# First-layer queries, decayed products and decay rows in DRAM tiles of their own, 2 KB per partition

## The chip, the cores and the metric

The kernel runs on one core of one Trainium2 chip. The metric is the device time of one execution in microseconds (us). For the kernel before, three runs gave 1664.18 us as the median, 1661.94 to 1669.47.

## The reference, cut to what matters

Three blocks work on 512 tokens (16 meta tokens ahead of them) of width 1024: a gated delta-rule layer, a latent-attention layer, and a layer of pooling, dilated attention and a feed-forward part. The change touches the first layer alone. It has 8 query/key heads of 128 features, each shared by 2 of the 16 value heads. In chunks it computes

```
gc = jnp.cumsum(g, axis=-1)
decay = jnp.exp(jnp.where(incl, gc[..., :, None] - gc[..., None, :], -jnp.inf))
attn = jnp.einsum('bhnid,bhnjd->bhnij', q, k) * decay
...
v_new = u_c - jnp.einsum('bhcd,bhde->bhce', w_c, state)
o_c = jnp.einsum('bhcd,bhde->bhce', qd_c, state) + jnp.einsum('bhij,bhje->bhie', a_c, v_new)
state = state * gl_c[..., None, None] + jnp.einsum('bhcd,bhce->bhde', kd_c, v_new)
```

The queries `q`, the decayed products `attn` and the rows of `gc` that `decay` is made from are what the change stores elsewhere. In the kernel a chunk is 128 tokens: chunk 0 holds the 16 meta tokens, chunks 1 to 4 the others.

## The kernel before, in words

Every projection is a product in three passes (high and low halves of both sides, lines 68, 71 and 72) that accumulates in PSUM tiles `pj_t`. Its weights come in units of 128x1024 floats (512 KB) from DRAM through line 115, and ScalarE (line 78) and VectorE (line 79) cut them in two. `first_layer` works in this order: gates and keys, half of the output gates, the 8 query heads, the 16 value heads, the other output gates, and then `core`, the recurrence over the chunks.

Nearly all loads and stores are issued by SyncE, which takes them in one fixed order. What stands in that order behind a transfer that waits, waits too. The order of each engine comes from a scheduler at build time. Side work (Gram products, decayed products, joins) runs as generators that are stepped with a budget between the halves of a projection (`column_tiles`, `bg.run`).

**Decay rows.** `decay_rows` (line 798) transposes `gc` into 80 rows of 128 floats (5 chunks by 16 heads) and stores them as `row_a`, one after another. Later `scores` (line 1093) loads, for each query head and each pair of chunks, the rows of its 2 value heads in both chunks to all 128 partitions at once (`fetch`, line 1100; tile `bca`). In `row_a` the two heads of a chunk are neighbours, and the two chunks lie 8 KB apart.

**Decayed products.** `products` masks `bca` on GpSimd (line 1109), takes exponents on ScalarE (line 1115), multiplies queries by keys on TensorE (`gq`, line 1117), joins both on VectorE (line 1118), and the result goes to DRAM (line 1129), in two pieces per partition: those of each chunk stand in another slab of `item_dram`. There are 2 such rounds per head, 16 in all. `bca` has 4 buffers (pool `ew`, tag `bc`), so the fifth load waits until the first store has landed.

**Queries.** `query_norm` (line 1079) stores each head's queries, four pieces of 128 floats per partition, into the same slabs (line 1080).

**Items.** `item_dram[u]` so holds for head `u` and chunk `c` one slab of 128 partitions by 768 floats: values and keys (384, line 1151), decayed products (256), queries (128). In `core` the stage `prepare` (line 1220) fetches such a slab in one transfer (line 1224) into one of 5 `item` buffers. `from_state` uses its queries two turns later (`ks`, line 1295), `new_values` follows, and `update` uses keys and decayed products (lines 1325 and 1333). A turn handles one of 32 pairs of chunk and head; the load of a turn waits for line 1325 of the item five turns before. `update` also loads the gates `sz` (line 1338). From the 24th turn on the next layer's output projection fills TensorE beside it.

```
stages = ((prepare, 0), (from_state, 2), (new_values, 3), (update, 4), (gated, 7))
```

Of the kernel before, what the change touches and what calls it, by code (L numbers as in the profile page):

```python
# [12 lines left out]
F32 = mybir.dt.float32  # L13
# [7 lines left out]
P = 128  # L21
D = 1024
KT = 8
META = 16
SEQ = 512
# [195 lines left out]
def tile_model(ctx, tc, a, out):  # L221
# [64 lines left out]
    with ExitStack() as mixed:  # L286
        ghi, glo, core = first_layer(e, mixed)
        mix = Mix(e, mixed, "w_out0", 2, None, "post0", HALVES, ghi, glo, (a["x0"], a["x1"]))
        half = mix.first_half()
        core(half)  # L290
        for _ in half:
            pass
        second = Second(e)
        mix.run(second)
# [255 lines left out]
def first_layer(e, mixed):  # L550
    tc, nc, a, dram, pj, wts, bg, ident, ones, vcol = (
        e.tc, e.nc, e.a, e.dram, e.pj, e.wts, e.bg, e.ident, e.ones, e.vcol
    )
    sz_dram = dram.tile([16, P, T1], F32, name="sz_dram")

    item_dram = [dram.tile([5, P, 6 * P], F32, name=f"item_dram{u}") for u in range(8)]
    row_a = dram.tile([80, P], F32, name="row_a")
    row_b = [dram.tile([40, P], F32, name=f"row_b{i}") for i in range(2)]

    left, right = ExitStack(), ExitStack()  # L560
# [25 lines left out]
    for i, s in enumerate(HALVES):  # L586
        x = flat[:, KT * s.start:KT * s.stop].rearrange("p (k t) -> p k t", k=KT)
# [164 lines left out]
    u = gs.tile([P, 5, 32], F32, name="u")  # L752
# [45 lines left out]
    def decay_rows():  # L798
        ra = gs.tile([80, P], F32, tag="ra", name="ra")
        ps = tr_tile([P, P], "ra_ps")  # L800
        nc.tensor.transpose(ps[0:80], gc.rearrange("p c h -> p (c h)"), ident)
        nc.vector.tensor_copy(ra, ps[0:80])
        nc.sync.dma_start(row_a, ra)
        nc.sync.dma_start(bc0, row_a[0:16, 0:META].partition_broadcast(META))

    one = gs.tile([P, 31], F32R, name="one")
    zero = gs.tile([P, 31], F32, name="zero")
# [5 lines left out]
    def square_sums(src, j, n, then):  # L813

        sq = cv.tile([P, T1], F32, tag="sq", name="sq")
        sqhi = cv.tile([P, T1], F32R, tag="sqhi", name="sqhi", bufs=1)
        sqlo = cv.tile([P, T1], F32R, tag="sqlo", name="sqlo", bufs=1)
        nc.scalar.activation(sq, src, AF.Square)
        cut(nc, sqhi, sqlo, sq)

        def sums():
            if j == 0:
                ss_t[0] = psm.tile([2 * n, CUT], F32, tag="ss", name="ss")
            for i, s in enumerate(HALVES):
                at = j + n * i
                for x in (sqhi, sqlo):
                    nc.tensor.matmul(
                        ss_t[0][:, 0:s.stop - s.start], lhsT=one[:, 15 - at:15 - at + 2 * n], rhs=x[:, s],
                        start=(at == 0 and x is sqhi), stop=(at == 2 * n - 1 and x is sqlo), skip_group_check=True,
                    )  # L830
            if j == n - 1:
                rows = gs.tile([2 * n, CUT], F32, tag="ssr", name="ssr")
                nc.scalar.activation(rows, ss_t[0], AF.Copy)
                side.add(1.5, lambda: columns(rows))

        def columns(rows):
            ps = tr_tile([P, 5, 2 * n], "ss_c")
            for c in range(5):
                t = win(c).start
                i = t >= CUT  # L840
                t -= HALVES[i].start
                nc.tensor.transpose(ps[:, c], rows[:, t:t + P], ident[0:2 * n, 0:2 * n])
            for cs, i in ((slice(0, 3), 0), (slice(3, 5), 1)):
                then(cs, ps[:, cs, n * i:n * i + n])

        side.add(SUMS, sums)
# [230 lines left out]
    bc0 = gs.tile([META, 16, META], F32, name="bc0")  # L1077

    def query_norm(kh, qT):
        nc.sync.dma_start(  # L1080
            item_dram[kh][1:5, :, 5 * P:].rearrange("c p t -> p c t"), qT[:, META:].rearrange("p (c t) -> p c t", t=P)
        )
        bg.add(scores(kh, qT), P_EARLY)

        def then(cs, ps):
            nc.vector.tensor_scalar(
                out=qe[:, :, cs].rearrange("p k c -> p c k"), in0=ps, scalar1=P * EPS, scalar2=P * EPS * EPS,
                op0=ALU.mult, op1=ALU.add,
            )

        square_sums(qT, kh, 8, then)

    def scores(kh, qT):

        hs = slice(2 * kh, 2 * kh + 2)
        rows = row_a.rearrange("(c h) i -> c h i", h=16)

        def fetch(c):
            bc = ew.tile([P, 2, 2, P], F32, tag="bc", name="bca")
            nc.sync.dma_start(  # L1100
                bc.rearrange("p j h i -> p j (h i)"),
                rows[c:c + 2, hs].rearrange("c h i -> c (h i)").partition_broadcast(P),
            )
            return bc

        def products(ex, rows, cs, n):
            ps = gr_tile([P, 2, P], "gq")
            for j, c in enumerate(cs):
                nc.gpsimd.affine_select(
                    out=ex[:, j], in_=rows[:, j], pattern=[[0, 2], [1, n]], compare_op=ALU.is_ge,  # L1110
                    fill=NEG, base=0, channel_multiplier=-1,
                )
                for r in range(2):
                    h = 2 * kh + r
                    nc.scalar.activation(ex[:, j, r], ex[:, j, r], AF.Exp, bias=col[0:n, c, h:h + 1])
                ts = slice(CHUNKS[c][0], CHUNKS[c][0] + n)
                nc.tensor.matmul(ps[0:n, j, 0:n], lhsT=kT[:, kh, ts], rhs=qT[:, ts], start=True, stop=True)
            nc.vector.tensor_tensor(
                out=ex, in0=ps[0:n, 0:len(cs), 0:n].unsqueeze(2).broadcast_to([n, len(cs), 2, n]), in1=ex, op=ALU.mult
            )  # L1120

        todo = (1, 3)
        ahead = deque(fetch(c) for c in todo)
        products(at0[:, hs].unsqueeze(1), bc0[:, hs].unsqueeze(1), (0,), META)
        yield 0.3, 0
        for c in todo:
            ex = ahead.popleft()
            products(ex, ex, (c, c + 1), P)
            nc.sync.dma_start(
                item_dram[kh][c:c + 2, :, 3 * P:5 * P].rearrange("c p a -> p c a"), ex.rearrange("p c r i -> p c (r i)")  # L1130
            )
            yield 2 * PRODUCT + 0.15, 0

    def token_rows(u, vT, c):
# [22 lines left out]
    def gates_later():  # L1157
        side.add(2.0, gates)
        side.add(10.0, cumulate)
        side.add(14.0, decay_rows)  # L1160
# [59 lines left out]
    def prepare(c, u):  # L1220
        o = live[c, u] = Env()
        item = ahead.tile([P, 6, P], F32, tag="item", name="item", bufs=5)
        o.vb, o.at, o.q = item[:, 0:3], item[:, 3:5], item[:, 5]
        nc.sync.dma_start(item.rearrange("p a d -> p (a d)"), item_dram[u][c])

    nothing = lambda: None
    keys = [conv_silu(("w_k", kh), 8 + kh, kT[:, kh], K_BUDGET, lambda kh=kh: key_norm(kh)) for kh in range(2)]
# [18 lines left out]
    for kh in range(8):  # L1246
        qT = cv.tile([P, T1], F32, tag="vT", name="qT", bufs=5)
        column_tiles(conv_silu(("w_q", kh), kh, qT, Q_BUDGET, lambda kh=kh, qT=qT: query_norm(kh, qT)))
# [23 lines left out]
    for i in range(5):  # L1272
        prepare(1, i)
# [68 lines left out]
    def gated(c, u):  # L1342
# [12 lines left out]
        cut(nc, ghi[i][:, us, ts], glo[i][:, us, ts], o.sz[:, :, 0:n], engine=nc.gpsimd)  # L1355

    stages = ((prepare, 0), (from_state, 2), (new_values, 3), (update, 4), (gated, 7))
    last = stages[-1][1]

# [854 lines left out]
```

## Time and profile before

| | us |
|---|---|
| median of three runs | 1664.18 |
| the profiled execution, its own time | 1664.66 |
| span of the profiled execution (first to last instruction) | 1662.8 |
| TensorE busy | 1585.1 |
| VectorE busy | 985.6 |
| ScalarE busy | 834.5 |
| GpSimd busy | 434.2 |

All times in the rows below count from the start of the span. A DMA's landing is counted from its issue on SyncE. The granted clock is the share of TensorE's full speed that the chip granted over a stretch, 1.00 being the upper of its two levels (2.4 GHz) throughout.

### The profile page before, as it was taken

To read this page: it belongs to the slowest core of one execution; us is meant where nothing else is said; L and a number is where in the kernel's file an instruction comes from. 1 tells how busy PE (TensorE), PEld (TensorE's weight loads), DVE (VectorE), ACT (ScalarE), POOL (GpSimd) and SP (SyncE) were. 2 spreads that over 40 slices of the span, in tenths; PEclk is the share of its full clock that TensorE was granted. 3 is DMA by queue.
4 is the path that set the end of the run, shared out by engine and by line. 5 is a ranking of instruction groups with operands and counts; after the bars stand their busy time and mean duration, and the time that the engine had idled before them with its cause. 6 is when DMAs were issued, how large, how long until landed. Compare 5 with 4: busy or idle time off the path is not lost.

```text
span 1662.8 us, 32878 instructions
## 1 busy us (share of the span) xinstructions
PE 1585.1 (95%) x12564; PEld 1452.0 (87%) x12564; DVE 985.6 (59%) x1988; ACT 834.5 (50%) x1998; POOL 434.2 (26%) x640
## 2 busy tenths in 40 slices
PE   6999879999999999999999999999999999999997
PEld 6999768888889999878999899988889888888997
DVE  6847758655376477785676623767855645544133
ACT  4886645554487564434666533435864432332230
POOL 1112110111186631222444312324544111111110
PEclk9999979999999999999999999999999999999998
DMA  3247874424465563455221223485624223223332
GB/s 131 101 163 211 210 139 135 112 95 156 129 184 186 170 242 125 146 199 162 74 61 52 71 100 129 134 253 179 154 65 139 90 101 101 89 101 107 97 115 76
DMA packets 133361, 219.72 MB, mean 132 GB/s; under 512 B 35988, under 2 KB 81364, under 8 KB 133076
## 3 DMA queue, kind: packets, MB, share of 16 engines
q1 hardware_dynamic: 126436, 204.83, 39.7%
q10 hardware_dynamic: 6768, 12.79, 2.2%
q8 instruction: 99, 1.62, 0.4%
q14 instruction: 58, 0.48, 0.1%
HBM read 173.81 MB, written 42.45 MB: 130 GB/s over the span
## 4 chain that ended last, share of the span: by engine, by line
PE 74%; DMA 10%; DVE 6%; ACT 4%; issue 4%; POOL 1%; SPq 0%; POOLq 0%; ACTq 0%; DVEq 0%
PE pj_t L68 20%; PE pj_t L71 19%; PE pj_t L72 19%; DMA bca<-row_a 2%; DMA item_dram<-bca 1%; DVE wlo L79 1%; DMA bc<-row_b 1%; DMA raw<-w_z 1%; PE ptr L1729 1%; ACT whi L78 1%; PE first L68 1%; PE first L71 1%; PE sc L68 1%; PE first L72 1%; PE vtp L1143 1%
## 5 line engine op out<-in xcount | busy, mean ns | idle before, releaser
L79 DVE TENSOR_TENSOR wlo<-raw,whi 128x1024 fp32r<-128x1024 f32 (+2 forms) x218 | 291.2, 1336 | 226.6 <-ACT whi L78 222.8
L78 ACT ACTIVATE whi<-raw 128x1024 fp32r<-128x1024 f32 (+3 forms) x225 | 232.3, 1033 | 337.7 <-PE pj_t L71 190.0
L68 PE MATMUL pj_t<-hhi,whi 128*128 128x272 f32 (+2 forms) x760 | 224.9, 297 | 6.4 <-ACT y L726 2.3
L71 PE MATMUL pj_t<-hlo,whi 128*128 128x272 f32 (+2 forms) x760 | 224.8, 296 | 0.0
L72 PE MATMUL pj_t<-hhi,wlo 128*128 128x272 f32 (+2 forms) x760 | 224.0, 295 | 0.0
L68 PEld LDWEIGHTS pj_t<-hhi,whi 128*128 128x128 f32 (+1 forms) x760 | 145.8, 192 | 10.0 <-issue 2.6
L72 PEld LDWEIGHTS pj_t<-hhi,wlo 128*128 128x128 f32 (+1 forms) x760 | 145.8, 192 | 4.9 <-issue 4.3
L71 PEld LDWEIGHTS pj_t<-hlo,whi 128*128 128x128 f32 (+1 forms) x760 | 146.1, 192 | 2.5 <-issue 1.7
L72 PE MATMUL pj_t<-x3hi,wlo 128*128 128x512 f32 x320 | 125.4, 392 | 0.0
L71 PE MATMUL pj_t<-x3lo,whi 128*128 128x512 f32 x320 | 125.2, 391 | 0.0
L68 PE MATMUL pj_t<-x3hi,whi 128*128 128x512 f32 x320 | 125.2, 391 | 0.0
L361 POOL TENSOR_TENSOR acc<-acc,ysq 128x256 f32<-128x256 f32 (+1 forms) x48 | 59.1, 1231 | 195.5 <-ACT ysq L359 195.4
L68 PE MATMUL pj_t<-ahi,whi 128*128 128x256 f32 x352 | 99.3, 282 | 0.0
L72 PE MATMUL pj_t<-ahi,wlo 128*128 128x256 f32 x352 | 99.1, 282 | 0.0
L71 PE MATMUL pj_t<-alo,whi 128*128 128x256 f32 x352 | 99.1, 282 | 0.0
L1404 POOL TENSOR_SCALAR p<-p,st 128x144 f32<-128x144 f32 (+3 forms) x112 | 61.7, 553 | 133.4 <-DVE st L1403 98.3
L2104 POOL TENSOR_TENSOR gt<-gt,x3rs 128x512 f32<-128x512 f32 x22 | 30.9, 1405 | 192.9 <-DVE gt L2103 192.9
L68 PE MATMUL pj_t<-ghi,whi 128*128 128x272 f32 (+1 forms) x256 | 75.3, 294 | 0.0
L1395 ACT ACTIVATE p<-p,st 128x144 f32<-128x144 f32 (+3 forms) x112 | 63.1, 564 | 23.1 <-DVE st L1390 21.1
L730 DVE SCALAR_TENSOR_TENSOR y<-xpad,fixed,y 128x528 f32<-128x528 f32 x96 | 74.1, 774 | 0.6
L71 PE MATMUL pj_t<-glo,whi 128*128 128x272 f32 (+1 forms) x256 | 72.8, 284 | 0.0
L72 PE MATMUL pj_t<-ghi,wlo 128*128 128x272 f32 (+1 forms) x256 | 72.8, 285 | 0.0
(549 smaller groups left out, 4729.7 us busy)
## 6 DMA issues: line engine op xcount, KB each, us to landing
raw<-w_out SPq DMA_DIRECT2D x54, 512.0 KB, 3.7
raw<-w_z SPq DMA_DIRECT2D x32, 512.0 KB, 3.4
item<-item_dram SPq DMA_DIRECT2D x32, 384.0 KB, 3.1
raw<-w_v SPq DMA_DIRECT2D x22, 512.0 KB, 4.1
raw<-w_gate SPq DMA_DIRECT2D x22, 512.0 KB, 3.3
raw<-w_up SPq DMA_DIRECT2D x22, 512.0 KB, 3.2
sz<-sz_dram SPq DMA_DIRECT2D x64, 128.0 KB, 2.7
raw<-w_down SPq DMA_DIRECT2D x16, 512.0 KB, 3.6
```

The lines of the kernel that those rows point to most:

```text
L68: first = nc.tensor.matmul(ps, lhsT=whi, rhs=xhi, start=start, stop=False)
L71: nc.tensor.matmul(ps, lhsT=whi, rhs=xlo, start=False, stop=False)
L72: nc.tensor.matmul(ps, lhsT=wlo, rhs=xhi, start=False, stop=stop)
L78: nc.scalar.activation(hi, src, AF.Copy)
L79: (engine or nc.vector).tensor_tensor(out=lo, in0=src, in1=hi.bitcast(F32), op=ALU.subtract)
L361: eng.tensor_tensor(out=acc[:, s], in0=acc[:, s], in1=sq[:, :n], op=ALU.add)
L730: nc.vector.scalar_tensor_tensor(out=y, in0=xpad[:, j:j + T1], scalar=cw[:, tap0, j:j + 1], in1=y, op0=ALU.mult, op1=ALU.add)
L1143: nc.tensor.transpose(tp[:, r], vT[r][:, win(c)], ident)
L1395: nc.scalar.activation(p[:, :at], p[:, :at], AF.Exp, bias=st[:, len(sc) - 1:len(sc)], scale=-1.0, accum_out=st[:, 3:4])
L1404: nc.gpsimd.tensor_scalar(out=p[:, :n], in0=p[:, :n], scalar1=st[:, 2:3], scalar2=factor, op0=ALU.mult, op1=ALU.mult)
L1729: nc.tensor.transpose(tr[:, k], p[:, META + P * k:META + P * k + P], ident)
L2104: nc.gpsimd.tensor_tensor(out=gt, in0=gt, in1=rs, op=ALU.mult)
```

## The change: what it does

`item_dram` keeps values and keys only. Decayed products go to `at_dram`, where a partition's two chunks and two heads stand together (2 KB); queries go to `q_dram`, 2 KB per partition and head; and `row_a` is laid out so that what one `fetch` reads is one piece of 2 KB. The meta tokens' rows get a tile `row_0`. In exchange the store of the decay rows becomes five transfers, and `prepare` fetches an item in three transfers: values and keys (192 KB), decayed products (128 KB), queries (64 KB).

```
-    item_dram = [dram.tile([5, P, 6 * P], F32, name=f"item_dram{u}") for u in range(8)]
-    row_a = dram.tile([80, P], F32, name="row_a")
+    item_dram = [dram.tile([5, P, 3 * P], F32, name=f"item_dram{u}") for u in range(8)]
+    at_dram = dram.tile([8, 2, P, 2, 2, P], F32, name="at_dram")
+    q_dram = dram.tile([8, P, SEQ], F32, name="q_dram")
+    row_0 = dram.tile([16, P], F32, name="row_0")
+    row_a = dram.tile([8, 2, 2, 2 * P], F32, name="row_a")
...
-        nc.sync.dma_start(row_a, ra)
-        nc.sync.dma_start(bc0, row_a[0:16, 0:META].partition_broadcast(META))
+        nc.sync.dma_start(row_0, ra[0:16])
+        for c in range(4):
+            nc.sync.dma_start(
+                row_a[:, c // 2, c % 2].rearrange("k (r i) -> k r i", r=2), ra[16 + 16 * c:32 + 16 * c]
+            )
+        nc.sync.dma_start(bc0, row_0[:, 0:META].partition_broadcast(META))
...
-        nc.sync.dma_start(
-            item_dram[kh][1:5, :, 5 * P:].rearrange("c p t -> p c t"), qT[:, META:].rearrange("p (c t) -> p c t", t=P)
-        )
+        nc.sync.dma_start(q_dram[kh], qT[:, META:])
...
             nc.sync.dma_start(
-                bc.rearrange("p j h i -> p j (h i)"),
-                rows[c:c + 2, hs].rearrange("c h i -> c (h i)").partition_broadcast(P),
+                bc.rearrange("p j h i -> p (j h i)"),
+                row_a[kh, c // 2].rearrange("j x -> (j x)").partition_broadcast(P),
             )
...
-            nc.sync.dma_start(
-                item_dram[kh][c:c + 2, :, 3 * P:5 * P].rearrange("c p a -> p c a"), ex.rearrange("p c r i -> p c (r i)")
-            )
+            nc.sync.dma_start(at_dram[kh, c // 2], ex)
...
-        nc.sync.dma_start(item.rearrange("p a d -> p (a d)"), item_dram[u][c])
+        nc.sync.dma_start(item[:, 0:3].rearrange("p a d -> p (a d)"), item_dram[u][c])
+        nc.sync.dma_start(o.at, at_dram[u, (c - 1) // 2, :, (c - 1) % 2])
+        nc.sync.dma_start(o.q, q_dram[u][:, P * (c - 1):P * c])
```

In the stage of the query heads SyncE's order stays as it is; only the shapes change. The rows of before begin with the fourth load of decay rows (`bca` as target is a load of decay rows, as source a store of products; `qT` is a store of queries, `w_v` a weight unit, `nn` a load of another part):

```order
L1100 DMA bca<-row_a 128x2x256
L1080 DMA item_dram_82<-qT 128x4x128
L115 DMA raw<-w_v 128x1024
L1129 DMA item_dram_81<-bca 128x2x256
L1080 DMA item_dram_83<-qT 128x4x128
L982 DMA nn<-d_in_2142 128x496
```

The same place after the change:

```order
L1103 DMA bca<-row_a 128x512
L1087 DMA q_dram<-qT 128x512
L115 DMA raw<-w_v 128x1024
L1132 DMA at_dram<-bca 128x512
L1087 DMA q_dram<-qT 128x512
L989 DMA nn<-d_in_2149 128x496
```

The order is the same, and each row's two or four pieces per partition have become one.

In `core` the order on SyncE, with what each issue waits for (`DMAHW` names are eight counters that the transfers take in turn, so that one waits for the one eight before it; `PE` is the release of the item's buffer, `Pool` that of the gates' buffer), is before:

```order
L1224 DMA item<-item_dram_84 128x768 [waits DMAHW3_49,PE_49]
L1338 DMA sz<-sz_dram 128x2x128 [waits DMAHW4_49,Pool_49]
L1224 DMA item<-item_dram_85 128x768 [waits DMAHW5_49,PE_49]
L1338 DMA sz<-sz_dram 128x2x128 [waits DMAHW6_49,Pool_49]
L1224 DMA item<-item_dram_86 128x768 [waits DMAHW7_49,PE_49]
```

and after the change:

```order
L1225 DMA item<-item_dram_86 128x384 [waits DMAHW5_49,PE_49]
L1226 DMA item<-at_dram 128x256 [waits DMAHW6_49]
L1227 DMA item<-q_dram 128x128 [waits DMAHW7_49]
L1341 DMA sz<-sz_dram 128x2x128 [waits DMAHW0_49,Pool_49]
L1225 DMA item<-item_dram_87 128x384 [waits DMAHW1_49,PE_49]
L1226 DMA item<-at_dram 128x256 [waits DMAHW2_49]
```

A turn issues four transfers in place of two. Only the first of an item waits for the buffer, the queries go out last, and eight transfers back is two turns back in place of four.

## Rows read from the trace of the kernel before

**Rows 1.** The page, busy time of each engine, share of the span

```profile
PE 1585.1 (95%) x12564; PEld 1452.0 (87%) x12564; DVE 985.6 (59%) x1988; ACT 834.5 (50%) x1998; POOL 434.2 (26%) x640
```

**Rows 2.** Busy time by stretch: us, each engine's busy time (instructions), granted clock, DMA share, GB/s

```profile
150.00:176.00 26.00, 25.50 (x212) 24.81 (x211) 24.39 (x42) 22.55 (x61) 9.73 (x16) 1.00 0.78 191
176.00:262.00 86.00, 64.77 (x577) 60.27 (x576) 51.70 (x98) 44.34 (x111) 11.58 (x35) 0.88 0.70 171
216.00:226.00 10.00, 6.67 (x32) 6.13 (x32) 4.79 (x9) 3.23 (x10) 0.77 (x2) 0.64 0.76 108
397.00:420.00 23.00, 23.00 (x193) 20.60 (x192) 8.81 (x16) 9.47 (x26) 2.10 (x6) 1.00 0.63 210
458.00:505.00 47.00, 45.04 (x276) 38.66 (x274) 33.44 (x103) 40.49 (x171) 40.67 (x85) 1.00 0.61 185
505.00:560.00 55.00, 54.44 (x409) 52.70 (x408) 31.36 (x69) 37.64 (x123) 37.08 (x62) 1.00 0.57 185
```

**Rows 3.** What TensorE waited for, 150 to 260 us: us in total, times, longest

```profile
PE ss L827 <- ACT sqhi L78: 9.5, 3, 3.8
PE gq L1117 <- DVE bca L1118: 8.1, 5, 2.6
```

**Rows 4.** Chain that ended last, 150 to 262 us: start, us, what

```profile
183.25 8.36 DMA item_dram<-bca
...
206.28 10.35 DMA item_dram<-bca
216.65 9.08 DMA bca<-row_a
```

**Rows 5.** What SyncE's queue waited for, 150 to 260 us

```profile
SPq L1100 <- DMA item_dram<-bca: 37.0, 10, 8.4
```

**Rows 6.** DMA issues, 186 to 262 us: KB each, median us to landing

```profile
item_dram<-bca SPq DMA_DIRECT2D x13, 256.0 KB, 7.7
bca<-row_a SPq DMA_DIRECT2D x11, 256.0 KB, 6.1
item_dram<-qT SPq DMA_DIRECT2D x5, 256.0 KB, 7.1
```

**Rows 7.** DMA issues, 136 to 160 us

```profile
bc<-row_b SPq DMA_DIRECT2D x10, 256.0 KB, 3.9
bca<-row_a SPq DMA_DIRECT2D x1, 256.0 KB, 5.3
```

**Rows 8.** DMA issues of the whole span

```profile
sz_dram<-zt SPq DMA_DIRECT2D x16, 264.0 KB, 4.2
sz_dram<-zr ACTq DMA_DIRECT2D x16, 256.0 KB, 2.1
```

**Rows 9.** SyncE's timeline, 150 to 180 us

```profile
177.16 0.47 SPq L1100 DMA_DIRECT2D bca<-row_a  x1
```

**Rows 10.** Tile `bca`, all its loads: count, durations, first and last start

```profile
L1100 SPq DMA_DIRECT2D bca<-row_a x16: 359/360/482, 156.8 to 242.5; - x16
```

**Rows 11.** Chain that ended last, 490 to 510 us

```profile
496.63 2.97 DMA item<-item_dram
499.65 0.70 PE ks L1295 x2
...
501.44 0.45 PE sp L1325 x2
501.91 3.29 DMA item<-item_dram
```

**Rows 12.** DMA issues, 460 to 505 us

```profile
item<-item_dram SPq DMA_DIRECT2D x17, 384.0 KB, 3.0
```

**Rows 13.** What TensorE waited for, 458 to 505 us

```profile
PE ks L1295 <- DMA item<-item_dram: 1.3, 7, 0.2
```

**Rows 14.** DMA issues, 300 to 306 us

```profile
nu<-ud SPq DMA_DIRECT2D x4, 64.0 KB, 2.2
```

**Rows 15.** SyncE's timeline, 450 to 460 us

```profile
453.78 2.09 SPq L1338 DMA_DIRECT2D sz<-sz_dram  x4
```

More of the change, by code (lines that the diff above doesn't have):

```diff
@@ L1095, in scores @@
         hs = slice(2 * kh, 2 * kh + 2)
-        rows = row_a.rearrange("(c h) i -> c h i", h=16)
         def fetch(c):
```

## The prediction

> **What bounds the kernel now.** I read the page first: TensorE is busy 95% of the span [rows 1], so a change of transfers can only win where TensorE stands idle or runs below full clock. The table of stretches shows where. From 150 to 176 us TensorE is busy 25.50 of 26 us, beside VectorE at 24.39 and ScalarE at 22.55, so that three nearly full engines do go together here. From 176 to 262 us, the query heads, it is busy 64.77 of 86 us at a granted clock of 0.88 [rows 2]. That stretch holds 86 − 64.77 = 21.2 us of idle time, and 64.77 × 0.12 = 7.8 us of slow clock (0.64 from 216 to 226 us, after idle time, a mix of the levels 1.2 and 2.4 GHz): 29.0 us at most. The reader should next see why. TensorE waits for the squares and the decayed products of VectorE and ScalarE [rows 3], but the chain goes through them to loads and stores of 8 to 10 us [rows 4], and SyncE's queue stands 37.0 us at the loads of decay rows until a store of decayed products has landed and frees one of four buffers [rows 5]. So the stretch is a loop: load of decay rows, mask, exponent, product, store, then the load four rounds later.
>
> Why are the transfers so slow? In that stretch a load of 256 KB takes 6.1 us, the stores 7.7 and 7.1 us [rows 6]. Between 136 and 160 us, in one mix of traffic, ten loads of the same kind (256 KB, one row to 128 partitions) take 3.9 us where the row is one piece of 2 KB (`bc`), and one takes 5.3 us where it is two pieces of 1 KB that lie 8 KB apart (`bca`) [rows 7]. And from 216 to 226 us, with two such loads in flight, the DMA engines are busy 0.76 of the time and move 108 GB/s, against 191 GB/s at 0.78 before [rows 2]. The loads in two pieces hold up what is queued behind them, the stores and weights too.
>
> The second place is the recurrence. From 458 to 505 us the chain runs through item loads: a load of 2.97 us, `ks` that waits for it, TensorE's work to the release of the next buffer, and again a load: 501.91 − 496.63 = 5.28 us for two turns [rows 11]. Seventeen items in 45 us are 2.65 us a turn, 5.29 for two [rows 12], so this loop has no slack there, and GpSimd with 40.67 of 47 us is little behind [rows 2].
>
> **The loop of the query heads.** The fourth load starts at 177.16 us [rows 9], the sixteenth and last at 242.5 [rows 10]: twelve steps in 65.3 us, 5.44 us each, and 4 × 5.44 = 21.8 us once around. Transfers take 6.1 + 7.7 = 13.8 of it [rows 6]; 8.0 us are the work between them. After the change the load has the shape of `bc`: 3.9 us, by the row in the same traffic [rows 7]. Ends: 2.1 us, the quickest 256 KB seen [rows 8], and 6.1, no change. The store of products becomes 2 KB per partition, nearest to the gates' store of 264 KB with 2,112 bytes per partition: 4.2 us [rows 8]; ends 2.1 and 7.7. The loop is then 3.9 + 8.0 + 4.2 = 16.1 us, 4.03 a step, a gain of 12 × (5.44 − 4.03) = 16.9 us. TensorE sets a floor under it: a head has 48 products of its projection, 10 for keys and 4 for squares, 31 matmuls a step, at 26.00/212 = 0.123 us each [rows 2] 3.8 us. At the floor the gain is 12 × (5.44 − 3.8) = 19.7 us, and with the idle tail after the last load 29.0, the ceiling above. I take 23 us: between the floor's 19.7 and the ceiling, since the 8.0 us of work hold slow clock and engines that waited behind each other, and since the stretch before shows three engines nearly full. What is late next is the row of VectorE's work: 51.70 us in the stretch [rows 2], within the 63 us that I leave to it.
>
> The queries' store goes from four pieces to one; it lands in 7.1 us now [rows 6], nobody needs it for 200 us, and its share of the queue is in the sum above.
>
> The Trainium skill, "DMA: Bandwidth & Descriptors", section Specifications, speaks against all this: it wants at least 512 bytes per piece for line rate, and all three transfers have that already. By that rule nothing is gained here, and the sum would end at the case "no faster load" below; the trace disagrees so far, 5.3 against 3.9 us [rows 7].
>
> **The decay rows' store.** Five transfers in place of one, and four more issues on SyncE, 2.09 us for four by the gates' row [rows 15]. Behind them stand the meta rows' load, first read by head 0 some 80 us later, and a weight unit that is loaded two units ahead: 0 us, and at most 2.1 if that cover were gone.
>
> **The items.** SyncE issues 32 × 2 = 64 more transfers. Four issues in a row take 2.09 us, 0.52 each [rows 15], so the queries, needed first and issued last, start 1.04 us later. A transfer of 64 KB lands 2.2 us after its issue [rows 14]: 1.04 + 2.2 = 3.2 us in place of 3.0 [rows 12]. Were the pieces of 512 bytes as slow as the whole item, 1.04 + 3.0 = 4.0. In the loop of two turns that is +0.2 to +1.0 us, and 17 items are 8.5 loops: +1.7 to +8.5 us. Below that: TensorE's wait for items is 1.3 us in all now [rows 13], and as values, keys and products come in transfers of their own, up to that could come back. I take +3: the row of the same size, and a little for its place behind two others. From 505 to 560 us TensorE is busy 54.44 of 55 us with the output projection beside it [rows 2], which hides the rest; without that cover it would be another 6 loops, 1 to 6 us. The issues on SyncE, 4 × 0.52 = 2.1 of 2.65 us a turn, still fit, and the wait for the transfer eight before looks back two turns, 5.3 us, more than a landing takes.
>
> The first five items are fetched beside the last gates, now in 15 transfers: ten more issues, 5.2 us, in which a weight load and three stores stand behind them. TensorE is busy without a gap from 397 to 420 us [rows 2] with units cut ahead: 0 us, at most 5 without.
>
> **The sum.** −23 + 3 = −20 us against the profiled execution's own 1664.66 us: 1644.7, say 1645. That execution lies 0.5 us above the median of the runs, within their spread.
>
> **The rivals.** *Only the loads get faster* (the stores stay at 7.7 us, because it is the write into DRAM that is slow): the loop is 3.9 + 8.0 + 7.7 = 19.6 us, 4.9 a step, a gain of 12 × 0.54 = 6.5 us, less 3: 1661. For it: stores are the slower of the two [rows 6]. Against: they are issued behind slow loads, and the gates' stores outside this stretch take 4.2 us [rows 8].
>
> *No faster load* (128 partitions that read one row are slow in any shape, or the new layout doesn't come out as one piece): 1664.7 + 3 = 1668. Against it stand ten loads that take 3.9 us with the very shape that is built now [rows 7]. It is also the Trainium skill's rule above.
>
> *The split of the items eats the gain*, slower than before: if an item's three transfers land one after the other instead of side by side, the queries come after 3 × 2.2 = 6.6 us, +3.6 in each of 8.5 loops, 31 us, and the 6 loops of the stretch behind, which TensorE's work no longer covers in full, some 5 more: 1664.7 − 23 + 36 = 1678. It decides from 23/8.5 = 2.7 us more per loop, a landing of the queries after 5.7 us. For it: a chain with no slack. Against: four gates' loads are issued within 2.09 us [rows 15], and the four 64 KB transfers of another part land in 2.2 us each [rows 14]. In a sentence of its own: the Trainium skill, "DMA: Bandwidth & Descriptors", section Rules for kernel authors, asks to coalesce, as transfers under 64 KB are mostly overhead, and the queries' load is just 64 KB; by it the split should cost, and no row here shows such a split.
>
> **How the numbers follow.** The forecast has 0.80, its own ends being 1635 (the whole 29.0, items at nothing) and 1657 (a gain of 16, items at 8.5). Only the loads: 0.10. No faster load: 0.06. Slower: 0.04. The ends hold some nine in ten of the forecast, 0.72, and the range 1635 to 1661 adds the first rival to them. About 0.5%, 8 us, is what a measurement can tell from no change: faster is below 1656. The forecast gives 0.79 to faster and 0.01 to the same; the first rival and the second go to the same, 0.16 together, less 0.02 where the first gains more than I reckon. Faster 0.81, same 0.15, slower 0.04.
>
> **What would show it.** Right: `bca` loads near 4 us and their stores near 4, SyncE's wait at the loads below 15 us in place of 37, the stretch that was 86 us at about 63 with a clock above 0.95, and turns of the recurrence at 2.65 to 2.85 us with the queries landing about 2.2 us after their issue. Wrong: `bca` still above 5 us, stores still above 7 with short loads, or `ks` waiting for the queries by more than 1 us a turn.

## The result, and the profile after

| | before | changed |
|---|---|---|
| median of four runs each, us | 1663.06 | 1641.61 |
| the profiled execution, its own time, us | 1664.66 | 1642.25 |
| its span, us | 1662.8 | 1640.5 |
| mean granted clock | 0.983 | 0.995 |

The ratio is 0.9865, its 95% interval 0.984 to 0.989: 21.5 us faster. Chips differ, so every run below is given as a ratio to the kernel before on the same chip.

The page of the changed kernel, busy time of each engine, answers to [rows 1]:

```profile
PE 1572.9 (96%) x12564; PEld 1440.3 (88%) x12564; DVE 987.5 (60%) x1988; ACT 834.7 (51%) x1998; POOL 440.6 (27%) x640
```

Its table of stretches, with the columns of [rows 2] (query heads, last gates, recurrence):

```profile
176.00:240.00 64.00, 58.05 (x580) 54.00 (x578) 53.00 (x98) 44.42 (x111) 14.48 (x35) 1.00 0.74 234
373.00:400.00 27.00, 27.00 (x225) 24.54 (x223) 12.26 (x22) 12.41 (x32) 2.87 (x7) 1.00 0.60 185
436.00:485.00 49.00, 42.92 (x260) 36.50 (x260) 32.28 (x99) 39.34 (x166) 39.31 (x81) 1.00 0.59 169
```

The same 580 products (577 before, [rows 2]) take 64 us in place of 86. Of these 22 us, 21.2 − 5.95 = 15.3 are idle time that went, and 64.77 − 58.05 = 6.7 are TensorE's own time at a granted clock of 1.00 in place of 0.88. The row from 373 to 400 us shows TensorE without a gap beside the last gates.

DMA issues of the changed kernel, 186 to 240 us (KB each, median us to landing), answering to [rows 6]:

```profile
at_dram<-bca SPq DMA_DIRECT2D x13, 256.0 KB, 4.5
bca<-row_a SPq DMA_DIRECT2D x11, 256.0 KB, 3.5
q_dram<-qT SPq DMA_DIRECT2D x5, 256.0 KB, 5.0
```

What SyncE's queue waited for, 150 to 240 us, answering to [rows 5]:

```profile
SPq L1103 <- DMA at_dram<-bca: 22.5, 10, 3.6
```

What TensorE waited for in the same time, answering to [rows 3]:

```profile
PE ss L834 <- ACT sqhi L78: 2.6, 2, 1.4
PE gq L1120 <- DVE bca L1121: 1.7, 2, 1.5
```

The chain of the changed kernel, 150 to 240 us, answering to [rows 4]:

```profile
183.69 5.96 DMA at_dram<-bca
189.71 4.45 DMA bca<-row_a
...
199.07 3.53 DMA bca<-row_a
...
208.64 3.90 DMA at_dram<-bca
```

Loads, stores and TensorE's waits all shrank: 6.1 to 3.5, 7.7 to 4.5, and 9.5 + 8.1 to 2.6 + 1.7 us. The 3.5 and the 4.5 rest on little, though: in this trace the landing of one of the eleven loads and of four of the thirteen stores is recorded. Two other times are there for every round. From a load's issue to GpSimd's first mask on its buffer it took 6.2 us before and takes 3.8 now (median of all 16 loads); from a store's issue to the issue of the load that reuses its buffer it took 7.9 and takes 5.5 (median of 12). Both are differences of starts on SyncE's and GpSimd's timelines, and upper bounds of the landings, as a mask or a load can wait for something else too. The chain, with loads of 4.45 and 3.53 us and stores of 5.96 and 3.90, is nearer to these. The fourth load of decay rows now starts at 178.54 us and the sixteenth at 224.91: twelve steps of 3.86 us, where [rows 9, 10] gave 5.44.

In the recurrence TensorE has 42.92 busy of 49 us, where it had 45.04 of 47 [rows 2]. DMA issues of the changed kernel, 436 to 485 us, answering to [rows 12]:

```profile
item<-item_dram SPq DMA_DIRECT2D x17, 192.0 KB, 2.2
item<-at_dram SPq DMA_DIRECT2D x17, 128.0 KB, 2.1
item<-q_dram SPq DMA_DIRECT2D x16, 64.0 KB, 2.7
```

What TensorE waited for there, answering to [rows 13]:

```profile
PE ks L1298 <- DMA item<-q_dram: 5.5, 10, 1.5
```

The chain of waits there, answering to [rows 11]:

```profile
466.87 0.32 SPq L1225
...
467.24 0.42 SPq L1226
...
467.71 2.74 DMA item<-q_dram
...
470.50 0.70 PE ks L1298 x2
...
472.29 0.45 PE sp L1328 x2
...
472.76 0.32 SPq L1225
...
473.60 2.21 DMA item<-q_dram
```

Two issues stand ahead of the queries' load on the path: 467.71 − 466.87 = 0.84 us. The loop of two turns takes 472.76 − 466.87 = 5.89 us here, against 5.28 in [rows 11].

What the recurrence costs as a whole can be read on SyncE's timeline, from the first load of an item in the loop to the load of the next part's residual. Before:

```profile
458.62 2.69 SPq L1224 DMA_DIRECT2D item<-item_dram  x2
...
577.83 0.42 SPq L373 DMA_DIRECT2D resid<-x  x1
```

After:

```profile
436.45 0.33 SPq L1225 DMA_DIRECT2D item<-item_dram  x1
436.83 0.44 SPq L1226 DMA_DIRECT2D item<-at_dram  x1
437.31 0.43 SPq L1227 DMA_DIRECT2D item<-q_dram  x1
...
560.23 0.43 SPq L373 DMA_DIRECT2D resid<-x  x1
```

577.83 − 458.62 = 119.2 us before and 560.23 − 436.45 = 123.8 after: the split gives back 4.6 us. By the start of one and the same TensorE instruction in both traces, the changed kernel is 21.4 us ahead at the end of the query heads (262 us of the kernel before), 18.9 at 300 us, 22.2 just ahead of the recurrence and 17.6 behind it; at the end of the span it is 22.3 ahead.

### The profile page after: what moved, and what is told of

It is laid out like the page before. It is cut to its first block, busy times and chain, and to the rows that moved or that the text cites. A ratio compares the mean times of both kernels' runs of the same rounds, so it can differ in the third digit from the quotient of the medians.

```text
span 1640.5 us, 32980 instructions
## 1 busy us (share of the span) xinstructions
PE 1572.9 (96%) x12564; PEld 1440.3 (88%) x12564; DVE 987.5 (60%) x1988; ACT 834.7 (51%) x1998; POOL 440.6 (27%) x640
## 4 chain that ended last, share of the span: by engine, by line
PE 74%; DMA 8%; DVE 7%; ACT 4%; issue 4%; SPq 1%; POOL 1%; POOLq 0%; DVEq 0%; ACTq 0%
PE pj_t L68 20%; PE pj_t L71 19%; PE pj_t L72 19%; DMA item<-q_dram 1%; DVE wlo L79 1%; DMA raw<-w_z 1%; PE ptr L1732 1%; ACT whi L78 1%; DVE y L403 1%; DMA resid<-h_w_out 1%; DMA at_dram<-bca 1%; PE sc L68 1%; ACT bc L915 1%; PE ks L1298 1%; PE vtp L1144 1%
```

## The experiments

The first four ran on one chip, 5 to 8 on a second, 9 to 11 on a third, 12 on a fourth. Table 1 gathers what the runs show of the query heads. Load and store are median landings of the stretch 186 to 240 us, 262 in before; in the rows changed, 1, 5, 10 and 12 they rest on one load and three or four stores each, in the others on six or more. The two columns behind them hold for every round: from a load to the first mask on it (median of 16), and from a store to the load that reuses its buffer (median of 12). A step is a twelfth of the time from the fourth to the sixteenth load of decay rows. Distances in KB are counted from the start of one piece to the start of the other.

**Table 1**

| kernel | two pieces of decay rows | load, us | store of products, us | load to mask, us | store to next load, us | step, us | ratio |
|---|---|---|---|---|---|---|---|
| before | 8 KB apart | 6.1 | 7.7 | 6.2 | 7.9 | 5.44 | 1 |
| changed | adjacent | 3.5 | 4.5 | 3.8 | 5.5 | 3.86 | 0.9865 |
| 1 rows alone | adjacent | 3.6 | 5.2 | 4.2 | 5.9 | 4.21 | 0.9842 |
| 2 all but rows | 8 KB | 6.9 | 7.5 | 6.7 | 7.6 | 5.33 | 1.0009 |
| 5 | 512 bytes between | 4.0 | 4.5 | 4.4 | 5.7 | 3.98 | 0.983 |
| 9 | 8.5 KB | 6.2 | 6.5 | 6.4 | 6.6 | 4.69 | 0.999 |
| 10 | 4 KB | 3.4 | 6.5 | 4.5 | 6.1 | 4.11 | 0.992 |
| 11 | 16 KB | 6.9 | 7.5 | 6.8 | 7.5 | 5.23 | 1.005 |
| 12 | 4 KB, table shifted | 3.5 | 4.9 | 4.3 | 5.6 | 3.98 | 0.993 |

Numbers 5 and 9 to 12 are one execution each, so their ratios are rough; their landings and steps are what they were run for.

**1. The rows alone.** The kernel before, with only the decay rows laid out anew; items stay whole, stores in their old pieces.

```
-    row_a = dram.tile([80, P], F32, name="row_a")
+    row_0 = dram.tile([16, P], F32, name="row_0")
+    row_a = dram.tile([8, 2, 2, 2 * P], F32, name="row_a")
...
```

> The kernel before with the new layout of the decay rows alone: products and queries still go into the item slabs in pieces of 1 KB and 512 bytes, an item is still one transfer. Theory (the loads in two pieces 8 KB apart hold up everything queued behind them): the loads land in about 3.5 us, the stores fall with them to 4 to 5 us although their pieces are unchanged, the query heads gain about 21 us, and with no split in the recurrence the whole comes out at 1637 to 1643, at or below the changed kernel. Rival (the stores are slow by themselves): loads 3.5, stores still near 7.7 us, a gain of 6 to 8 us, 1655 to 1658.

Measured: 1646.44 us against 1671.40, ratio 0.9842 (0.9808 to 0.9875). The loads fell, and the stores, which nobody reshaped, fell with them:

```profile
item_dram<-bca SPq DMA_DIRECT2D x12, 256.0 KB, 5.2
bca<-row_a SPq DMA_DIRECT2D x11, 256.0 KB, 3.6
item_dram<-qT SPq DMA_DIRECT2D x5, 256.0 KB, 6.0
```

The columns are those of [rows 6], stretch 186 to 240 us. From the first item load of the recurrence (439.04 us) to the residual's (558.97) it is 119.9 us, as before. So this part alone gives the whole gain and costs nothing later.

**2. All but the rows.** The changed kernel, with the decay rows as they were.

```
-    row_a = dram.tile([8, 2, 2, 2 * P], F32, name="row_a")
+    row_a = dram.tile([80, P], F32, name="row_a")
...
-                bc.rearrange("p j h i -> p (j h i)"),
-                row_a[kh, c // 2].rearrange("j x -> (j x)").partition_broadcast(P),
+                bc.rearrange("p j h i -> p j (h i)"),
+                rows[c:c + 2, hs].rearrange("c h i -> c (h i)").partition_broadcast(P),
```

> The changed kernel with the old layout of the decay rows: products and queries in pieces of 2 KB, items in three transfers, loads of decay rows still in two pieces 8 KB apart. Theory: loads still 5.5 to 6 us, stores behind them still 6 to 7 us, the query heads gain 0 to 4 us, the recurrence costs 3 to 5, the whole 1660 to 1668. Rival (stores are slow by themselves): stores at 4 us, half of the gain or more, 1650 to 1655.

Measured: 1672.64 us, ratio 1.0009 (0.9989 to 1.0029). The same stretch:

```profile
bca<-row_a SPq DMA_DIRECT2D x9, 256.0 KB, 6.9
at_dram<-bca SPq DMA_DIRECT2D x9, 256.0 KB, 7.5
q_dram<-qT SPq DMA_DIRECT2D x5, 256.0 KB, 7.4
```

Stores of one 2 KB piece per partition stay at 7.5 and 7.4 us as long as the loads ahead of them are slow. The recurrence takes 588.40 − 461.38 = 127.0 us, 7.8 more than before. By the same TensorE instructions run 2 is 0.9 us ahead of the kernel before at 262 us, where run 1 is 19.2 ahead. Runs 1 and 2 show together which part is worth what: the rows carry the gain, the two other tiles bring next to nothing by themselves.

**3. The split alone.** The kernel before, each item fetched in three transfers out of the same slab.

```
-        nc.sync.dma_start(item.rearrange("p a d -> p (a d)"), item_dram[u][c])
+        whole = item.rearrange("p a d -> p (a d)")
+        for s in (slice(0, 3 * P), slice(3 * P, 5 * P), slice(5 * P, 6 * P)):
+            nc.sync.dma_start(whole[:, s], item_dram[u][c, :, s])
```

> The kernel before with only the fetch of an item cut in three transfers, each from the same slab as before (values and keys, products, queries). Theory: the split costs what the changed kernel lost in the recurrence, 4 to 5 us: 1666 to 1669. Rival (the loss there comes from the new places in DRAM, 512 byte pieces out of rows of 2 KB): no loss, 1662 to 1665.

Measured: 1676.82 us, ratio 1.0031 (1.0014 to 1.0048), and 587.68 − 460.73 = 127.0 us for the recurrence, +7.7. TensorE's waits from 460 to 508 us:

```profile
PE ks L1297 <- DMA item<-item_dram: 7.9, 7, 2.5
```

It was 1.3 us in all in [rows 13]. The split costs 5 us of the whole by the ratio, whatever tile the parts come from. The Trainium skill, "DMA: Bandwidth & Descriptors", section Rules for kernel authors, says to coalesce small transfers; here the trace agrees, with the queries' 64 KB landing in 2.7 us where 384 KB took 3.0 [rows 12].

**4. The queries first.** The changed kernel, the three loads of an item in another order.

```
+        nc.sync.dma_start(o.q, q_dram[u][:, P * (c - 1):P * c])
         nc.sync.dma_start(item[:, 0:3].rearrange("p a d -> p (a d)"), item_dram[u][c])
         nc.sync.dma_start(o.at, at_dram[u, (c - 1) // 2, :, (c - 1) % 2])
-        nc.sync.dma_start(o.q, q_dram[u][:, P * (c - 1):P * c])
```

> The changed kernel with the queries fetched first of an item's three transfers instead of last. Theory (the product with the state waits for the queries, which start about 0.9 us late): that wait falls from 5.5 us to about 1, the recurrence gets back 2 to 4 us, 1637 to 1640. Rival (another wait, for values or products, takes its place, or the four issues on SyncE are the cost): within 1 us of the changed kernel, 1640 to 1643.

Measured: 1651.86 us, ratio 0.9869 (0.9846 to 0.9893): no gain over the changed kernel, a miss. The queries did land sooner, 1.9 us after their issue. But the build put TensorE's work in another order, and the chain from 436 to 485 us shows what that made of the loop:

```profile
438.23 1.93 DMA item<-q_dram
440.20 0.70 PE ks L1298 x2
440.89 0.45 PE sp L1328 x2
441.36 1.92 DMA item<-q_dram
443.32 0.70 PE ks L1298 x2
444.02 0.45 PE sp L1328 x2
444.48 1.81 DMA item<-q_dram
```

`sp`, the last reader of an item's buffer, now stands right behind `ks`, and the loop is one turn instead of two: load, `ks`, `sp`, next load, 441.36 − 438.23 = 3.13 us. Every turn's load is on the path now. The term I priced (0.85 us of issues) was gone, and another wait had taken its place.

**5. Pieces, not place.** The changed kernel, the two 1 KB pieces of a load again apart, with 512 bytes between them.

```
-    row_a = dram.tile([8, 2, 2, 2 * P], F32, name="row_a")
+    row_a = dram.tile([8, 2, 2, 3 * P], F32, name="row_a")
...
-                row_a[kh, c // 2].rearrange("j x -> (j x)").partition_broadcast(P),
+                row_a[kh, c // 2, :, 0:2 * P].partition_broadcast(P),
```

> The changed kernel, but the decay rows of one load are again two pieces of 1 KB per partition, now 512 bytes apart in place of 8 KB. Theory A (the distance of 8 KB between the pieces makes the loads slow): loads near 3.5 to 4 us as in the changed kernel, the query heads as short as there, within 3 us of the changed kernel. Theory B (pieces of 1 KB in place of 2 KB make them slow): loads at 5.3 to 6.6 us as before, most of the 22 us lost again.

Measured: loads of 4.0 us, 4.4 to the mask, and steps of 3.98 (Table 1), 1643.82 us against 1671.73. Two pieces of 1 KB are as good as one of 2 KB to within what two executions of the changed kernel differ by (steps of 3.86 and 4.08); so the number of pieces isn't what slowed the loads, the distance is.

**6. The changed kernel once more**, beside the runs 5, 7 and 8, without an edit (so no diff).

> The changed kernel once more, to stand on the same chip beside the others of this call: 1.2 to 1.5% below the kernel before; turns of the recurrence at 2.75 to 2.85 us.

Measured: 1649.17 us, ratio 0.9867 (0.9851 to 0.9882). The recurrence takes 563.51 − 437.24 = 126.3 us here, +7.1, with 3.13 us a turn over its first sixteen turns, longer than the 2.75 to 2.85 that I expected. The step in the query heads is 4.08: the size of both terms differs by some 3 us between two executions of one kernel.

**7. A tile for each part.** The changed kernel, the three parts of an item in buffers of their own, five each, queries first.

```
-        item = ahead.tile([P, 6, P], F32, tag="item", name="item", bufs=5)
+        o.q = ahead.tile([P, P], F32, tag="iq", name="iq", bufs=5)
+        o.vb = ahead.tile([P, 3, P], F32, tag="item", name="item", bufs=5)
+        o.at = ahead.tile([P, 2, P], F32, tag="iat", name="iat", bufs=5)
...
```

> The changed kernel with three tiles per item in place of one (queries, values and keys, products, 5 buffers each), queries fetched first. Their buffer is free as soon as the product with the state has read it, so their load waits no longer for the update. Theory (in the recurrence the chain runs from the release of the whole item through its load to the product with the state): the wait of that product for queries falls below 1.5 us in all, and the recurrence gets back the 4 to 5 us: 4 to 6 us below the changed kernel. Rival (four issues a turn on SyncE, or the engines' work, set the pace): within 2 us of the changed kernel.

Measured: 1639.25 us against 1671.73, ratio 0.9809 (0.9791 to 0.9827), against 1649.17 for the changed kernel on this chip: 9.9 us, more than the 4 to 6 that I expected. TensorE's waits from 430 to 480 us hold no load any more:

```profile
PE ks L1298 <- ACT qs L1306: 1.6, 5, 0.4
PE otp L1175 <- POOL vb L1217: 1.1, 1, 1.1
```

And the chain in that time runs through GpSimd, VectorE, ScalarE and TensorE, with no transfer in it:

```profile
442.94 0.70 POOL ms L1215
443.73 0.72 POOL o L1217 x2
444.45 0.70 POOL glo L79
445.51 0.72 POOL ms L1215
446.26 0.43 DVE o L1339
446.77 0.70 ACT qs L1213 x4
...
451.15 0.72 POOL ms L1215
```

The buffer of the queries comes free at `ks` and no longer waits for `sp` two turns on, so the next load goes out before it is needed. Number 4 has the same order of loads with one buffer for all three parts and gained nothing, so the buffers are what makes the difference; whether the build's order of TensorE's work has a part in it was not separated. Between 300 and 700 us this kernel gains a further 5.0 us on the kernel before, by the same TensorE instructions; the changed kernel gains 0.6. It has the lowest ratio of all kernels here.

**8. More buffers still.** Number 7 with six buffers for values and keys, and the products fetched two turns later.

```
-        o.vb = ahead.tile([P, 3, P], F32, tag="item", name="item", bufs=5)
+        o.vb = ahead.tile([P, 3, P], F32, tag="item", name="item", bufs=6)
...
+    def late(c, u):
+        o.at = ahead.tile([P, 2, P], F32, tag="iat", name="iat", bufs=3)
...
-    stages = ((prepare, 0), (from_state, 2), (new_values, 3), (update, 4), (gated, 7))
+    stages = ((prepare, 0), (late, 2), (from_state, 2), (new_values, 3), (update, 4), (gated, 7))
```

> The same three tiles, and in addition 6 buffers for values and keys and the products fetched two turns later into 3 buffers, so that values too are released a turn earlier than they are needed. Theory: no load of an item is on the chain any more, turns go down to what GpSimd and ScalarE allow, about 2.45 us for 2.75: 6 to 9 us below the changed kernel, the fastest of all. Rival: as for three tiles with 5 buffers, no further gain (values were never late).

Measured: 1640.78 us, ratio 0.9825 (0.9807 to 0.9843), 8.4 us below the changed kernel as expected, but no gain over number 7: the rival was right. The loads had left the path already, so moving them further is worth nothing; the shorter turn that I had hoped for didn't come.

**9 to 12. How far apart.** Number 5 with only the layout of the rows changed, always with two 1 KB pieces per load: 8.5 KB apart (9), 4 KB (10), 16 KB (11).

```
+    row_a = dram.tile([2, 2, 16 * P + P], F32, name="row_a")
...
+    row_a = dram.tile([2, 2, 2, 8 * P], F32, name="row_a")
...
+    row_a = dram.tile([2, 2, 32 * P], F32, name="row_a")
```

> The changed kernel with the two pieces of a load 8.5 KB apart (a pad of 512 bytes after each chunk's rows). Theory A1 (a distance of just 8 KB is what hurts, both pieces falling on the same part of the memory): loads near 3.6 us, as with 512 bytes between them. Theory A2 (any long distance hurts): loads at 5.3 to 6.6 us.

> The changed kernel with the two pieces of a load 4 KB apart. Theory A1 (a distance of just 8 KB): loads near 3.6 us. Theory A2 (longer is worse): loads between 3.6 and 6 us, the query heads between the two kernels.

> The changed kernel with the two pieces of a load 16 KB apart. Theory A1: if only a distance of 8 KB hurts, loads near 3.6 us; if its multiples hurt too, 5.3 to 6.6 us and the gain lost. Theory A2 (longer is worse): 5.3 us or more.

Measured: loads of 6.2, 3.4 and 6.9 us; to the mask 6.4, 4.5 and 6.8. The load's row of each, 186 to 240 us, first of 8.5 KB:

```profile
bca<-row_a SPq DMA_DIRECT2D x11, 256.0 KB, 6.2
```

then of 4 KB:

```profile
bca<-row_a SPq DMA_DIRECT2D x11, 256.0 KB, 3.4
```

and of 16 KB:

```profile
bca<-row_a SPq DMA_DIRECT2D x10, 256.0 KB, 6.9
```

With a distance that is no power of two (8.5 KB) the loads stay slow, so it is not the exact 8 KB alone that hurts. But 8.5 KB is better than 8 or 16: the step is 4.69 us against 5.44 and 5.23, and by the same TensorE instructions the query heads gain 9.1 us. Its ratio hides this, as its recurrence takes 578.42 − 449.45 = 129.0 us. The loads turn slow somewhere between 4 and 8 KB. The numbers 9 to 12 all store the rows in more than one transfer, as the changed kernel does, so that isn't what separates fast from slow. In number 12 the table begins 4 KB further on, so that the two pieces of a load lie on either side of what would have been a boundary of 8 KB within the table:

```
+    row_a = dram.tile([10, 8 * P], F32, name="row_a")
...
+                row_a[1 + 4 * (c // 2) + c % 2:5 + 4 * (c // 2) + c % 2:2].rearrange("a (k r i) -> a k r i", r=2, i=P), ra[16 + 16 * c:32 + 16 * c]
```

> The two pieces of a load 4 KB apart once more, but the whole table shifted by 4 KB, so that if it starts on a multiple of 8 KB each pair of pieces lies in two neighbouring blocks of 8 KB in place of one. Theory B1 (a load whose pieces lie in different 8 KB blocks of DRAM is slow): loads at 5 to 6 us where the unshifted table gave 3.5. Theory B2 (the distance itself decides, somewhere between 4 and 8 KB): loads near 3.5 us again.

Measured: 3.5 us, 4.3 to the mask, as without the shift. So blocks of 8 KB within the table don't explain it; the distance does. Why a distance of 8 KB or more slows a load that 128 partitions make of one row stays open: the table's place in DRAM was not tried, nor any distance between 4 and 8 KB.

## Why the prediction was right, and where it was off

1645 us was forecast and 1641.61 measured, inside the range, in the forecast's own case.

*The loop of the query heads.* Right in its mechanism and its total. The load was put at 3.9 us from the `bc` rows [rows 7] and came to 3.5 in the one landing recorded, 3.8 to the mask; the step was put at 4.03 and came to 3.86. The gain was put at 23 and is 22 us by the stretch, or 21.4 by the offset at its end. The clock came back to 1.00 as expected.

The terms of a round were off, and part of the closeness is luck. Its 8.0 us of work were what two medians of landings left over. The same three rounds, from the fourth load to the eighth, twelfth and sixteenth, can be cut by the starts of loads, masks and stores instead (mean of the three, us):

| | load to mask | mask to store | store to next load | round |
|---|---|---|---|---|
| before, as predicted from | 6.1 | 8.0, all work | 7.7 | 21.8 |
| before, by starts | 7.1 | 5.3 | 9.4 | 21.8 |
| changed, as predicted | 3.9 | 8.0, all work | 4.2 | 16.1 |
| changed, by starts | 4.3 | 5.2 | 5.9 | 15.5 |

The work stayed the same, as was assumed, and the two transfers together gave 6.2 us a round where 5.7 were forecast. But there was less work and more transfer in the round than the sum had: the stores came out 1.7 us longer than forecast and the work 2.8 us shorter, and these cancel for the most part. The loop alone gave 12 × (5.44 − 3.86) = 19.0 us (16.9 in the sum); the rest of the 22 came outside these twelve steps. The 23 itself was chosen between a floor and a ceiling and not worked out.

The floor doesn't hold. It was 31 products a step at 0.123 us, 3.8 us. TensorE in the changed kernel, 178.5 to 224.9 us, the time of the twelve steps:

```profile
178.50:224.90 46.40, 40.55 (x319) 37.25 (x317) 37.49 (x73) 31.23 (x81) 11.87 (x27) 1.00 0.76 252
```

That is 26.6 products a step, 40.55 / 12 = 3.4 us, and number 8 has steps of 3.75 us. TensorE has 5.85 us idle in these steps, so it does not set them alone.

*The stores.* Their size was forecast as 4.2 us; it is 4.5 by four landings and at most 5.5 from store to next load. The price was taken from their new shape, one piece per partition in place of two, though the prediction also says that slow loads hold up the stores behind them. The second reason is the one that the runs bear out. Run 2 has the new pieces and 7.5 us; run 1 has the old ones and 5.2. They were slow mainly because of the slow loads. Between run 1 (steps of 4.21 us) and the two runs of the changed kernel (3.86 and 4.08) the new shape may be worth 12 × 0.13 to 12 × 0.35, that is 2 to 4 us, which the ratios don't separate from nothing. Whether anything else than the loads sets a store's time stays open: number 10 has stores of 6.5 us, but by three landings, and 6.1 from store to next load, between run 1 and number 9.

*The signs to look for.* I wanted SyncE's wait at the loads below 15 us and found 22.5. That number contradicted my own loop: as long as a load waits for the store four rounds back, some 10 of each round's 15.5 us are transfers and SyncE stands in them. What had to shrink was the longest wait (8.4 to 3.6 us) and TensorE's, and both did. The turn of the recurrence that I named, 2.65 to 2.85 us, was missed as well: the loop shown above has 5.89 us for two turns, and the first sixteen turns take 2.96 us each.

*The items.* +3 was forecast within +1.7 to +8.5, and this term was too small. +4.6 was measured here, +7.1 in number 6, +7.7 and +7.8 in the runs 3 and 2, +5.6 in number 4, and from +5.3 to +9.8 in the single executions of numbers 5 and 9 to 12. So the term was too small by 2 to 7 us; the execution profiled first is the cheapest of ten, and two of the ten lie outside the range. The issues were cheaper than the gates' row said, 0.84 us for two in place of 1.04, but the queries landed 2.7 us after their issue and not 2.2, and in some rounds 4 to 5 us: the chain has one of 4.20 us and number 6 one of 4.63. The row of four 64 KB transfers [rows 14] came from a stretch without gates and items beside it. The cost went the way of the slower rival, at an eighth to some quarter of its 36 us; that an item's transfers land one after the other, as that rival had it, isn't shown, and 2.7 us is far from its 6.6.

*The row store and the items fetched ahead.* 0, as said: TensorE has 27.00 busy of 27 us from 373 to 400 us, where the first items are fetched, and at 100 us, some 30 us behind the row store, the same TensorE instructions start at the same time as before.

*The rivals.* "No faster load" is out with loads of 3.5 us, 3.8 to the mask. The Trainium skill, "DMA: Bandwidth & Descriptors", section Specifications, asks for at least 512 bytes per piece. The traces show that this is not enough here: loads in pieces of 1 KB took 6.2 us at 8.5 KB apart and 3.4 at 4 KB, 6.4 and 4.5 to the mask. "Only the loads get faster" is out, and run 1 shows why it can't be had: the stores follow.

*Not forecast.* From 17.6 us behind the recurrence the lead grows to 22.3 at the end. Between 1100 and 1500 us run 2, which has no gain at all, also draws ahead by 2.8 us of the kernel before, so part of it lies in the profiled execution of before. No run isolates the rest.

## What to carry to other kernels

When transfers of one queue are all slow, find the one that leads it and mend that first: here the new layout of one small table carried a gain of 1.6% alone, and the tiles added beside it brought nothing that could be measured on top. Keep the pieces that one broadcast load reads close together in DRAM: up to 4 KB apart they were fast here, at 8 KB and more they were not. When a load is split, give each part its own buffer, or the part that is read first waits for the last reader of the whole. And before a median of landings goes into a sum, look how many landings it rests on, and cut the same time by the starts of its reader and its successor.

## What the runs showed that was not expected

A load of one row of 2 KB to 128 partitions takes 3.4 to 4.0 us (3.8 to 4.5 to the mask) with its two halves adjacent, 512 bytes between them or 4 KB apart, and 6.1 to 6.9 us (6.2 to 6.8) with 8, 8.5 or 16 KB. A transfer of 64 KB is hardly quicker than one of 384 KB in the same place: 2.7 against 3.0 us, 1.9 when it is issued first. And an order of three issues on SyncE, changed in the code, changed TensorE's order too, and with it the length of the loop: the recurrence in number 4 is to be read from its own chain, not from the edit.
